# Sending the 63-row group of a top-2 gating kernel ahead of the 65-row group

## The chip, the core and the metric

The kernel runs on one core of a Trainium2 chip. The metric is the device time of one execution in microseconds (us). Before the change the median of three runs is 240.05 us (240.04, 240.05 and 240.24).

## What is computed

For each of 16 x 1024 = 16,384 tokens there are 8 router logits and a row of 512 floats. The two largest logits give two weights, and the row is written out twice, once times each weight, the smaller weight first.

```python
def reference(x, router_logits, k):            # x 16x1024x512, logits 16x1024x8, k = 2
    probs = np.exp(router_logits - logits_max)
    probs = probs / np.sum(probs, axis=-1, keepdims=True)
    topk_indices = np.argsort(probs, axis=-1)[..., -k:]
    topk_probs = np.take_along_axis(probs, topk_indices, axis=-1)
    topk_probs = topk_probs / np.sum(topk_probs, axis=-1, keepdims=True)
    x_expanded = x[:, :, np.newaxis, :].repeat(k, axis=2)
    return (x_expanded * topk_probs[..., np.newaxis]).astype(np.float32)
```

So 33.55 MB of rows and 0.52 MB of logits are read, and 67.11 MB are written. Normalising two of the eight probabilities leaves a sigmoid of the difference of the two largest logits, which is how the kernel has it.

## The kernel before

The 16,384 tokens lie on 128 partitions, 128 tokens ("rows" from here on, 2 KB each) to a partition. They are taken in two groups, the first of 65 rows per partition, the second of 63 (`GROUPS`, L49). A group is a contiguous stretch of the tensors, so a partition's rows of one group are contiguous in HBM. There is one input buffer `xs` of 65 rows per partition, which serves both groups, and one output buffer `osp` of 16 rows (each twice, for the two weights).

**Loads.** `LOADS` (L51) cuts each group's load into pieces, issued on the SyncE (SP) queue by L112: 2, 4, 2, 8, 17 and 32 rows for the first group, 16, 16 and 31 for the second. After the first 6 rows the logits of both groups are loaded by two transfers (L116, L117), and the weights `WA` of all 128 rows are worked out at once by `top2_weights` (VectorE, then two sigmoids on ScalarE).

**Products.** For each step of a plan VectorE multiplies n rows by their two weights (L128) and the result is stored by one transfer (L136), again on SP; only the first step of 2 rows is stored from ScalarE's queue. The steps of a group, as (first row, rows, target), are:

- rows 0 to 15 into `osp` (in the first group as 2 and 14 rows, in the second as 16);
- rows 16 to 31, written over `xs` rows 0 to 31, which are spent by then;
- rows 32 to 39 into the lower half of `osp`, rows 40 to 47 into its upper half;
- the rest, from row 48 on, written over the last part of `xs`, by the helper `over`, whose first target row is a = 2r - G for a group of G rows: the doubled rows end at row G.

`LAST` (L54) cuts that rest. With G = 65 it is 9 rows at 48 (target rows 31 to 48) and 8 rows at 57 (target rows 49 to 64): the first of these touches row 31, which the store of rows 0 to 31 still reads, so it waits for that store. With G = 63 it is one step of 15 rows at 48, whose target is rows 33 to 62 and touches nothing that is being stored.

**Order.** VectorE runs its steps in the order of the plan. SP issues in the order of the program and a transfer that waits holds up all behind it: the loads of the first group, its stores, the loads of the second group, its stores. A load of the second group waits until the stores have read what it overwrites: the first for the store of `xs` rows 0 to 31, the second in addition for the 9-row store (row 31), the third for the last store.

Of the kernel before, what the change touches and what calls it, by code (L numbers as in the profile page):

```python
# [1 line left out]

# [4 lines left out]

F32 = mybir.dt.float32
ALU = mybir.AluOpType
ACTF = mybir.ActivationFunctionType  # L10
P = 128


def top2_weights(nc, pool, logits, M, E, tag=""):

    hi, lo, n = None, None, E  # L20
    while n > 1:
        n //= 2
        if hi is None:
            a, b = logits[:, :, 0:n], logits[:, :, n : 2 * n]
            nhi = pool.tile([P, M, n], F32, tag=f"hi{n}{tag}")
            nlo = b
            nc.vector.tensor_tensor(nhi, a, b, op=ALU.max)  # L27
            nc.vector.tensor_tensor(nlo, a, b, op=ALU.min)  # L28
        else:
            a, b = hi[:, :, 0:n], hi[:, :, n : 2 * n]  # L30
            nhi = pool.tile([P, M, n], F32, tag=f"hi{n}{tag}")
            nlo = pool.tile([P, M, n], F32, tag=f"lo{n}{tag}")
            tmp = pool.tile([P, M, n], F32, tag=f"tmp{n}{tag}")
            nc.vector.tensor_tensor(tmp, lo[:, :, 0:n], lo[:, :, n : 2 * n], op=ALU.max)  # L34
            nc.vector.tensor_tensor(nlo, a, b, op=ALU.min)  # L35
            nc.vector.tensor_tensor(nlo, nlo, tmp, op=ALU.max)  # L36
            nc.vector.tensor_tensor(nhi, a, b, op=ALU.max)  # L37
        hi, lo = nhi, nlo
    dlt = pool.tile([P, M], F32, tag=f"dlt{tag}")
    nc.vector.tensor_tensor(dlt, hi[:, :, 0], lo[:, :, 0], op=ALU.subtract)  # L40
    WA = pool.tile([P, M, 2], F32, tag=f"WA{tag}")
    nc.scalar.activation(WA[:, :, 0], dlt, ACTF.Sigmoid, scale=-1.0)  # L42
    nc.scalar.activation(WA[:, :, 1], dlt, ACTF.Sigmoid, scale=1.0)  # L43
    return WA

GROUPS = [65, 63]  # L49

LOADS = [[2, 4, 2, 8, 17, 32], [16, 16, 31]]  # L51


LAST = [[(48, 9), (57, 8)], [(48, 15)]]  # L54


@with_exitstack
def kernel(
    ctx: ExitStack,
    tc: tile.TileContext,  # L60
    x: bass.AP,
    router_logits: bass.AP,
    k: bass.AP,
    out: bass.AP,
):
    nc = tc.nc
    B, S, D = x.shape
    E = router_logits.shape[-1]
    N = B * S
    assert int(k) == 2 and E == 8 and N == P * sum(GROUPS)  # L70
    M = N // P

    L = 16
    x_v, o_v, rl_v = [], [], []
    t0 = 0
    for n in GROUPS:
        t1 = t0 + P * n
        x_v.append(
            x.rearrange("b s d -> (b s) d")[t0:t1].rearrange("(p m) d -> p m d", p=P)
        )  # L80
        o_v.append(
            out.rearrange("b s k d -> (b s) k d")[t0:t1].rearrange(
                "(p m) k d -> p m k d", p=P
            )
        )
        rl_v.append(
            router_logits.rearrange("b s e -> (b s) e")[t0:t1].rearrange(
                "(p m) e -> p m e", p=P
            )
        )  # L90
        t0 = t1

    wpool = ctx.enter_context(tc.tile_pool(name="wpool", bufs=1))
    logits = wpool.tile([P, M, E], F32)
    xs = wpool.tile([P, max(GROUPS), D], F32)
    osp = wpool.tile([P, L, 2, D], F32)

    def over(r, n, G):

        a = 2 * r - G
        return xs[:, a : a + 2 * n, :].rearrange("p (r k) d -> p r k d", k=2)

    h = L // 2
    e = 2
    m0 = 0
    for g, G in enumerate(GROUPS):
        r = 0  # L110
        for n in LOADS[g]:
            nc.sync.dma_start(xs[:, r : r + n, :], x_v[g][:, r : r + n, :])  # L112
            r += n
            if g == 0 and r == 6:

                nc.sync.dma_start(logits[:, :G], rl_v[0])  # L116
                nc.sync.dma_start(logits[:, G:], rl_v[1])  # L117
                WA = top2_weights(nc, wpool, logits, M, E)
        assert r == G
        begin = [(0, e, osp[:, :e]), (e, L - e, osp[:, e:])] if g == 0 else [(0, L, osp)]  # L120
        plan = begin + [
            (L, L, over(L, L, 2 * L)),
            (2 * L, h, osp[:, :h]),
            (2 * L + h, h, osp[:, h:]),
        ]
        plan += [(r, n, over(r, n, G)) for r, n in LAST[g]]
        for r, n, og in plan:
            nc.vector.tensor_tensor(  # L128
                og,
                xs[:, r : r + n, :].unsqueeze(2).to_broadcast([P, n, 2, D]),  # L130
                WA[:, m0 + r : m0 + r + n, :].unsqueeze(3).to_broadcast([P, n, 2, D]),
                op=ALU.mult,
            )

            queue = nc.scalar if n == e else nc.sync
            queue.dma_start(o_v[g][:, r : r + n], og)  # L136
        m0 += G


# [1 line left out]
_INS = ['x', 'router_logits', 'k']  # L141
_OUTS = [((16, 1024, 2, 512), 'float32')]

_NUMBERS = {'k': 2}


# [26 lines left out]
```

## Time and profile before

| quantity | value |
|---|---|
| median of three runs | 240.05 us |
| span of the profiled execution | 238.5 us |
| VectorE busy | 142.0 us, 60% of the span |
| share of the SP queue's transfers in the time of 16 DMA engines | 97.8% |
| share of ScalarE's queue in it | 1.0% |
| moved | 101.19 MB |
| multiply of 8 / 9 / 15 / 16 rows (L128) | 8.69 / 9.76 / 16.16 / 17.23 us |

The span is measured from the first to the last event that the profiler ascribes to the program; the time of a run includes some 1.5 us around it. A transfer's "us to landing" runs from its issue by the queue to the moment at which its semaphore is complete. In the timeline a line merges instructions of one kind: start, length, engine and line, what is written and read, and in brackets how long the engine had been idle and who ended that. "SPq" is the issuing sequencer of SyncE, "DVE" VectorE, "ACT" ScalarE.

### The profile page before, as it was taken

How to read it: one execution, taken by the hardware profiler on the slowest of the kernel's cores; microseconds unless marked ns; L12 is line 12 of the kernel's file. 1: busy time of each engine (PE TensorE's matmuls, PEld its weight loads, DVE VectorE, ACT ScalarE, POOL GpSimd, SP SyncE). 2: the span in 40 equal slices, each digit the busy share in tenths (PEclk: the TensorE clock that was granted, in tenths of full speed). 3: DMA queues.
4: the chain of work that ended last, by engine and by line, in shares of the span. 5: the costliest groups of instructions: out<-in, count | busy, mean ns of one | idle time of the engine just before them, and what ended most of it. 6: DMA issues, size and time to landing. Idle time of an engine off the chain costs nothing.

```text
span 238.5 us, 116 instructions
## 1 busy us (share of the span) xinstructions
DVE 142.0 (60%) x23; ACT 1.8 (1%) x3; POOL 0.2 (0%) x4
## 2 busy tenths in 40 slices
DVE  0599999900299699900000699999006999990000
ACT  2000000000000000000000000000000000000000
POOL 0000000000000000000000000000000000000000
DMA  7999989899898999999999999998999989999994
GB/s 261 434 470 411 459 383 528 330 462 462 352 506 352 440 440 440 440 414 465 440 429 434 412 478 458 394 495 374 462 418 429 451 363 429 440 440 429 495 453 206
DMA packets 3312, 101.19 MB, mean 424 GB/s; under 512 B 368, under 2 KB 496, under 8 KB 880
## 3 DMA queue, kind: packets, MB, share of 16 engines
q1 hardware_dynamic: 3168, 100.14, 97.8%
q10 hardware_dynamic: 144, 1.05, 1.0%
HBM read 34.08 MB, written 67.11 MB: 424 GB/s over the span
## 4 chain that ended last, share of the span: by engine, by line
DMA 43%; DVE 41%; issue 4%; SPq 1%; ACT 0%; DVEq 0%
DVE xs L128 22%; DVE osp L128 18%; DMA out_dram<-xs 15%; DMA xs<-in_x_dram 13%; DMA out_dram<-osp 13%; DMA logits<-in_router_logits_dram 3%; SPq L112 0%; DVE nhi L27 0%; DVE logits L28 0%; DVE nlo L36 0%; DVE nhi L37 0%; DVE tmp L34 0%; DVE nlo L35 0%; SPq L116 0%; SPq L136 0%
## 5 line engine op out<-in xcount | busy, mean ns | idle before, releaser
L128 DVE TENSOR_TENSOR osp<-xs,WA 128x8192 f32<-128x8192 f32 (+3 forms) x7 | 69.1, 9908 | 61.9 <-DMA xs<-in_x_dram 31.2
L128 DVE TENSOR_TENSOR xs<-xs,WA 128x16384 f32<-128x16384 f32 (+3 forms) x5 | 69.1, 13812 | 2.2 <-DMA out_dram<-xs 2.0
L27 DVE TENSOR_TENSOR nhi<-logits 128x512 f32<-128x512 f32 x1 | 0.7, 691 | 8.3 <-DMA logits<-in_router_logits_dram 8.3
L42 ACT ACT_TABLE_LOAD x1 | 1.3, 1283 | 0.7 <-PEq L154 0.7
L28 DVE TENSOR_TENSOR logits<-logits 128x512 f32<-128x512 f32 x1 | 0.7, 692 | 0.0
L37 DVE TENSOR_TENSOR nhi<-nhi 128x256 f32<-128x256 f32 (+1 forms) x2 | 0.7, 351 | 0.0
L35 DVE TENSOR_TENSOR nlo<-nhi 128x256 f32<-128x256 f32 (+1 forms) x2 | 0.7, 350 | 0.0
L36 DVE TENSOR_TENSOR nlo<-nlo,tmp 128x256 f32<-128x256 f32 (+1 forms) x2 | 0.7, 350 | 0.0
L34 DVE TENSOR_TENSOR tmp<-logits 128x256 f32<-128x256 f32 x1 | 0.4, 418 | 0.0
L42 ACT ACTIVATE WA<-dlt 128x128 f32<-128x128 f32 x1 | 0.3, 315 | 10.2 <-DVE dlt L40 10.2
L40 DVE TENSOR_TENSOR dlt<-nhi,nlo 128x128 f32<-128x128 f32 x1 | 0.3, 291 | 0.0
L43 ACT ACTIVATE WA<-dlt 128x128 f32<-128x128 f32 x1 | 0.3, 297 | 0.0
L34 DVE TENSOR_TENSOR tmp<-nlo 128x128 f32<-128x128 f32 x1 | 0.3, 283 | 0.0
L154 POOL MEMSET const-bfloat16-1.0<- 128x1 bf16 x1 | 0.1, 101 | 0.0
L154 POOL MEMSET const-uint8-127<- 128x1 uint8 x1 | 0.1, 101 | 0.0
L154 POOL MEMSET const-float32-0.0<- 128x1 f32 x1 | 0.1, 98 | 0.2 <-issue 0.2
L154 POOL MEMSET const-float32-1.0<- 128x1 f32 x1 | 0.1, 98 | 0.0
## 6 DMA issues: line engine op xcount, KB each, us to landing
out_dram<-osp SPq DMA_DIRECT2D x4, 4096.0 KB, 20.7
xs<-in_x_dram SPq DMA_DIRECT2D x2, 4096.0 KB, 29.9
xs<-in_x_dram SPq DMA_DIRECT2D x1, 7936.0 KB, 38.0
out_dram<-xs SPq DMA_DIRECT2D x1, 7680.0 KB, 23.2
out_dram<-osp SPq DMA_DIRECT2D x1, 7168.0 KB, 33.9
out_dram<-xs SPq DMA_DIRECT2D x1, 4608.0 KB, 20.4
xs<-in_x_dram SPq DMA_DIRECT2D x1, 4352.0 KB, 22.4
out_dram<-xs SPq DMA_DIRECT2D x1, 4096.0 KB, 21.5
```

Of the source, the lines that this page charges most:

```text
L27: nc.vector.tensor_tensor(nhi, a, b, op=ALU.max)
L28: nc.vector.tensor_tensor(nlo, a, b, op=ALU.min)
L34: nc.vector.tensor_tensor(tmp, lo[:, :, 0:n], lo[:, :, n : 2 * n], op=ALU.max)
L35: nc.vector.tensor_tensor(nlo, a, b, op=ALU.min)
L36: nc.vector.tensor_tensor(nlo, nlo, tmp, op=ALU.max)
L37: nc.vector.tensor_tensor(nhi, a, b, op=ALU.max)
L40: nc.vector.tensor_tensor(dlt, hi[:, :, 0], lo[:, :, 0], op=ALU.subtract)
L42: nc.scalar.activation(WA[:, :, 0], dlt, ACTF.Sigmoid, scale=-1.0)
L43: nc.scalar.activation(WA[:, :, 1], dlt, ACTF.Sigmoid, scale=1.0)
L128: nc.vector.tensor_tensor(og, xs[:, r : r + n, :].unsqueeze(2).to_broadcast([P, n, 2, D]), WA[:, m0 + r : m0 + r + n, :].unsqueeze(3).to_b ...
L154: nc = _bacc.Bacc("TRN2", target_bir_lowering=False, num_devices=1)
```

## The change

The two groups change places: 63 rows come first and 65 second. The lists that belong to a group go with it: `LAST` is swapped as it stands, so the 15-row step now ends the first group and the 9- and 8-row steps end the second. The loads of the first group are 2, 4, 2, 8, 16 and 31 rows, those of the second 16, 17 and 32. The number of transfers, the bytes and the number of VectorE instructions stay as they were.

```diff
-GROUPS = [65, 63]
+GROUPS = [63, 65]
 
-LOADS = [[2, 4, 2, 8, 17, 32], [16, 16, 31]]
+LOADS = [[2, 4, 2, 8, 16, 31], [16, 17, 32]]
 
 
-LAST = [[(48, 9), (57, 8)], [(48, 15)]]
+LAST = [[(48, 15)], [(48, 9), (57, 8)]]
```

## The prediction

> **What bounds the kernel now.** I read the page's head first, then windows of the span, then the timeline and the landings of the transfers, and the chain of waits last.
>
> ```profile
> span 238.5 us, 116 instructions
> DVE 142.0 (60%) x23; ACT 1.8 (1%) x3; POOL 0.2 (0%) x4
> ...
> q1 hardware_dynamic: 3168, 100.14, 97.8%
> q10 hardware_dynamic: 144, 1.05, 1.0%
> ...
> DMA 43%; DVE 41%; issue 4%; SPq 1%; ACT 0%; DVEq 0%
> ```
>
> VectorE has 40% of the span free; the two DMA queues together fill 98.8% of the time of 16 DMA engines. The windows (length, engines, granted clock, DMA share, GB/s) say where the rest is:
>
> ```profile
> 0.00:1.70 1.70, 0.00 (x0) 0.97 (x1) 0.20 (x4) 1.00 0.00 0
> 47.00:142.60 95.60, 45.62 (x6) 0.00 (x0) 0.00 (x0) 1.00 1.00 434
> 43.00:47.00 4.00, 4.00 (x1) 0.00 (x0) 0.00 (x0) 1.00 1.30 492
> 158.00:162.00 4.00, 4.00 (x1) 0.00 (x0) 0.00 (x0) 1.00 1.21 516
> 236.50:238.50 2.00, 0.00 (x0) 0.00 (x0) 0.00 (x0) 1.00 0.00 0
> ```
>
> Nothing moves in the first 1.7 us, then the engines are full to the end. Packets are booked where they start, so in a short window the figures run above 1.00; what tells is share per GB/s. In the long window it is 1.00 for 434. In 43 to 47, where the first group's loads give way to its stores, 492 GB/s should take 1.13 and take 1.30: (1.30 - 1.13) x 4.0 = 0.66 us of all engines lost. At the second such turn, 158 to 162, 516 should take 1.19 and take 1.21: 0.08 us.
>
> ```profile
> 64.02 17.29 DVE L128 TENSOR_TENSOR osp<-xs,WA 128x8192 f32<-128x8192 f32 x2 [16.71 <-DMA out_dram<-osp]
> 72.74 8.93 SPq L136 DMA_DIRECT2D out_dram<-osp  x2
> 83.36 18.48 DVE L128 TENSOR_TENSOR xs<-xs,WA 128x9216 f32<-128x9216 f32 x2 [2.05 <-DMA out_dram<-xs]
> ...
> 180.91 17.29 DVE L128 TENSOR_TENSOR osp<-xs,WA 128x8192 f32<-128x8192 f32 x2 [13.39 <-DMA out_dram<-osp]
> 189.63 8.93 SPq L136 DMA_DIRECT2D out_dram<-osp  x2
> 198.24 16.16 DVE L128 TENSOR_TENSOR xs<-xs,WA 128x15360 f32<-128x15360 f32 x1
> 214.42 0.33 SPq L136 DMA_DIRECT2D out_dram<-xs  x1
> ```
>
> Issue plus time to landing gives each transfer's landing:
>
> ```profile
> out_dram<-xs SPq DMA_DIRECT2D x1, 7680.0 KB, 23.2
> out_dram<-osp SPq DMA_DIRECT2D x1, 7168.0 KB, 33.9
> xs<-in_x_dram SPq DMA_DIRECT2D x1, 7936.0 KB, 38.0
> xs<-in_x_dram SPq DMA_DIRECT2D x1, 42.6
> ```
>
> The 32-row load lands at 4.4 + 42.6 = 47.0, the 14-row store at 30.07 + 33.9 = 63.9, and so on in the order of issue: 83.2, 92.9, 102.6, 113.5 (9 rows), 123.4, 132.9 (load of 16), 142.6, 161.4 (load of 31), 180.8, 200.2, 209.8, 219.5, and the last 15-row store at 214.4 + 23.2 = 237.6. From 47.0 to 237.6, 126 rows per partition are stored and 63 loaded, 82.6 MB in 190.6 us: 433 GB/s, the rate of the full window. So one row costs 0.605 us to load and 1.210 us to store, and no transfer there waits for its issue. The kernel is bound by bytes. The chain of waits books 41% on VectorE only because each store was released by VectorE; the engines were still on earlier bytes then.
>
> **What the change removes, adds and moves.** Bytes, the 23 transfers of SP and ScalarE, and the multiplies are the same before and after, so the stream costs what it cost, unless it runs dry. That has to be looked at transfer by transfer, from the row prices above and the multiplies of the profile.
>
> First group. The two logits transfers swap their sizes (260 and 252 KB); VectorE's first instruction waits for both, so nothing moves there. The loads end 2 rows earlier, 47.0 - 1.2 = 45.8. The 14-row store, ready at 30.1, lands at 62.7 (+16.9), the 16-row store (ready at 47.3) at 82.1 (+19.4). The landing at 62.7 frees `osp`; with the 0.08 us seen between landing (63.94) and start (64.02) VectorE does the two 8-row steps from 62.8 to 80.1 (17.29 as one group). Their stores are issued at 71.5 and 80.1, are reached at 82.1 and 91.7, and land at 91.7 and 101.4. Next comes the moved step of 15 rows. The 2.05 us wait that stood here belonged to the 9-row step, whose target includes `xs` row 31; rows 33 to 62 are in no transfer. So it starts at 80.13, ends 16.16 us later, and its store is issued at 96.3. The stream gets there at 101.4: a margin of 5.1 us, the thinnest of the new order.
>
> Does 5.1 suffice? The old kernel has the same place with the same margin: its 15-row store is issued at 214.4 while the store before it lands at 198.2 + 21.3 = 219.5, and it lands 18.1 us after that, exactly 15 x 1.210. No gap. The time from an issue to moving bytes is not shown under load; bounds are 1.0 us (first issue at 0.73, DMA share zero until 1.70) and 2.4 us (the first 512 KB load lands 3.6 us after its issue, of which 1.2 are its bytes). I take 1.0, with the engines running; with 2.4 the margin is still 2.7.
>
> The Trainium skill ("DMA: Bandwidth & Descriptors", section "Anatomy of one DMA — SWDGE (gpsimd) path") would speak against longer transfers that others wait for: it gives every DMA a fixed part of about 2.0 us on that path, mostly the receipt of the last write. Twelve stores would then pay 24 us if nothing hid it; here their landings follow each other at the price of their bytes alone, so it is hidden, and at 2.0 us the 15-row store would keep 3.1 us.
>
> The second group's loads. On SP they stand behind the 15-row store. The first (16 rows) waits for the 16-row store of `xs`, landed at 82.1, so it goes at once after 96.3 (before: 102.3, behind the 8-row store). The second (17 rows) overwrites rows 16 to 32, and row 32 was read by the 8-row step that ended by 71.5: no wait left, where before it stood until 113.5 for the 9-row store. The third (32 rows, 33 to 64) waits for the 15-row store: 101.4 + 18.1 = 119.6. Behind it on SP stand only stores that are not ready before 146. At 119.6 the queue holds 33 rows of loads, 20.0 us (before: 19.1 us, 142.6 - 123.5). Landings: 129.2, 139.5, 158.9.
>
> Second group. VectorE starts 0.12 us after the 129.2 landing (as 132.91 to 133.03) and needs 17.23 twice: stores issued at 146.6 and 163.8, reached at 158.9 and 178.3, landing at 178.3 and 197.6. The 8-row steps run from 178.4 to 195.7; their stores are reached at 197.6 and 207.3, 10.5 and 11.6 us after their issue, and land at 207.3 and 217.0. Now the 9-row step waits for row 31, until 197.6: from 195.7 that is 2.0 us, so the old wait is not removed but moved here. It ends at 207.5; the stream wants it at 217.0, 9.5 us later. The 8-row step is issued at 216.2, wanted at 227.9. Last landing: 217.0 + 10.9 + 9.7 = 237.6, as before.
>
> So of the moved parts, the 2.0 us wait, the earlier loads and the shorter last store (8 rows, 9.7 us, instead of 18.1) each come out at zero, covered by margins of 5.1 to 20 us of bytes already queued. Without that cover the dearest, the 15-row multiply, would show its whole 16.2 us. The sum is 237.6 for the last landing and the same 0.9 us behind it: span 238.5, and with the 1.55 us between span and median, 240.05.
>
> What is left is the ramp. From 1.75 to 47.0 pass 45.25 us for 65 rows loaded, 2 stored and 0.52 MB of logits, 18.6 MB or 43.0 us: 2.3 us are lost there, 0.66 of them at the turn. The change cuts these loads by one row in two places; I take this loss as it is, and price its part at the turn below.
>
> **Rivals.** First, faster: the chain of waits is right, and VectorE's path sets the end; then the 2.05 us ahead of 83.36 are gained, 238.0. For it speaks only the 41% of the chain; against it the landings spaced by bytes alone, and that the wait returns at 195.7.
>
> Second, faster: the turn from loads to stores in the first group loses 0.08 instead of 0.66, because its last load is now the 31-row one that turned cheaply at 158 to 162. 240.05 - 0.58 = 239.5. Against it: the turn at 158 was the second store stream on this queue, and being first may be the cause, which the change leaves.
>
> Third, slower: the reverse. The 32-row load, after which 0.66 us were lost, now stands ahead of the second group's stores at 158.9, and if that turn loses 0.66 in place of 0.08 while the first keeps its loss, 240.05 + 0.58 = 240.6. It decides as soon as more than 0.48 us is lost there beyond today's 0.08.
>
> Fourth, slower: the stream runs dry at 101.4. It begins to cost once the 15-row store is issued later than about 100.4 (101.4 less 1.0 us). If its multiply were held until the 8-row store ahead lands, at 91.7, it would be issued at 108.0 and cost 7.6 us: 247.6. Nothing in the targets makes it wait so.
>
> **How the numbers follow.** A difference of 0.2%, 0.48 us, is what a measurement can tell from none. No change, bound by bytes: 0.76, at 240.05, with a range of its own of 239.8 to 240.3. Second rival 0.08, first 0.03, third 0.09, fourth 0.04. The range reaches from 239.6 to 240.6, half into the second and third; beyond lies about 0.15. Faster 0.11, same 0.76, slower 0.13.
>
> **What would show it.** Right: DMA share still 1.00 at 434 GB/s from 47 to 236; the 15-row step without a wait ahead of it; 2.0 us of idle time on `xs` late in the second group, at about 196; the last landing at 237.6. Wrong: stores that land later than their bytes allow after the one before, above all the 15-row one (119.6) and the first after the 32-row load (178.3), or a share per GB/s above 1.00 for 434 at the second turn.

## The result and the profile after

The changed kernel takes 240.63 us (median of 22 runs, 240.13 to 242.12); the kernel before, measured beside it 22 times, 240.26 us (240.04 to 241.18). The ratio is 1.0021, 95% interval 1.0011 to 1.0031: slower by 0.2%, half a microsecond at the mean. The medians hide its shape. Of the changed kernel's runs 9 of 22 lie above 240.7 us, of the old one's 2 of 22, and the fastest runs are equal to 0.1 us. The change makes a slower outcome more frequent; it does not add the same amount to every run.

The page of one execution of the changed kernel, which took 241.0 us:

```profile
span 239.2 us, 114 instructions
...
DVE 142.0 (59%) x23; ACT 1.8 (1%) x3; POOL 0.2 (0%) x4
...
q1 hardware_dynamic: 3168, 100.14, 97.6%
q10 hardware_dynamic: 144, 1.05, 1.0%
```

Busy time, packets and bytes are those of before; the span is 0.7 us longer. The timeline around the two places that the prediction followed:

```profile
63.13 17.29 DVE L128 TENSOR_TENSOR osp<-xs,WA 128x8192 f32<-128x8192 f32 x2 [15.54 <-DMA out_dram<-osp]
71.85 8.94 SPq L136 DMA_DIRECT2D out_dram<-osp  x2
80.46 16.16 DVE L128 TENSOR_TENSOR xs<-xs,WA 128x15360 f32<-128x15360 f32 x1
96.64 0.33 SPq L136 DMA_DIRECT2D out_dram<-xs  x1
97.03 23.34 SPq L112 DMA_DIRECT2D xs<-in_x_dram  x3
...
198.49 18.48 DVE L128 TENSOR_TENSOR xs<-xs,WA 128x9216 f32<-128x9216 f32 x2 [2.03 <-issue]
208.27 9.06 SPq L136 DMA_DIRECT2D out_dram<-xs  x2
```

The 15-row step follows the 8-row steps without a wait, and the 2.0 us wait has moved to 198.49. Landings, from issue and time to landing (the 31-row load issued at 4.63; the 15-row store at 96.64; the loads of 16, 17 and 32 rows at 97.03, 98.05 and 120.04; the last store at 217.00):

```profile
xs<-in_x_dram SPq DMA_DIRECT2D x1, 7936.0 KB, 41.5
out_dram<-xs SPq DMA_DIRECT2D x1, 7680.0 KB, 23.4
xs<-in_x_dram SPq DMA_DIRECT2D x1, 4096.0 KB, 32.7
xs<-in_x_dram SPq DMA_DIRECT2D x1, 4352.0 KB, 42.0
xs<-in_x_dram SPq DMA_DIRECT2D x1, 39.7
out_dram<-xs SPq DMA_DIRECT2D x1, 4096.0 KB, 21.3
```

Against the forecast they are 46.1 (45.8), 120.0 (119.6), 129.7 (129.2) and 140.0 us (139.5); the 32-row load lands at 159.7 (158.9), the last store at 238.3 (237.6). So 0.3 us are lost by the end of the first loads, a little at 120, and 0.3 more between 140 and 159.7. From there on the 0.7 to 0.8 us stand unchanged for 78 us of stores.

Windows of the changed kernel (length, engines, granted clock, DMA share, GB/s), first three long enough to weigh share against rate, then some so short that each counts packets, booked where they start:

```profile
42.00:46.00 4.00, 4.00 (x1) 0.00 (x0) 0.00 (x0) 1.00 1.24 483
46.10:139.60 93.50, 44.69 (x5) 0.00 (x0) 0.00 (x0) 1.00 1.01 436
155.50:159.50 4.00, 4.00 (x1) 0.00 (x0) 0.00 (x0) 1.00 1.29 524
44.95:45.45 0.50, 0.50 (x1) 0.00 (x0) 0.00 (x0) 1.00 3.98 1720
45.70:45.80 0.10, 0.10 (x1) 0.00 (x0) 0.00 (x0) 1.00 1.33 573
158.25:158.90 0.65, 0.65 (x1) 0.00 (x0) 0.00 (x0) 1.00 3.50 1512
159.35:159.45 0.10, 0.10 (x1) 0.00 (x0) 0.00 (x0) 1.00 1.52 655
235.60:236.25 0.65, 0.00 (x0) 0.00 (x0) 0.00 (x0) 1.00 1.75 756
236.70:236.80 0.10, 0.00 (x0) 0.00 (x0) 0.00 (x0) 1.00 0.76 328
```

The same of before, where the first stores and the last store's last packets start:

```profile
46.15:46.66 0.51, 0.51 (x1) 0.00 (x0) 0.00 (x0) 1.00 4.17 1799
234.25:234.85 0.60, 0.00 (x0) 0.00 (x0) 0.00 (x0) 1.00 3.54 1536
234.85:235.05 0.20, 0.00 (x0) 0.00 (x0) 0.00 (x0) 1.00 0.71 307
```

The first turn loses (1.24 - 483/434) x 4.0 = 0.5 us of all engines (before 0.66), the second (1.29 - 524/434) x 4.0 = 0.3 (before 0.08). The short windows say who pays. The first store has packets of 57,344 bytes: 1720 GB/s x 0.50 us are 15 of them, and 573 x 0.10 one. Fifteen engines begin their stores by 45.45 us and one only at 45.7. At the second turn 15 begin by 158.90 and one after 159.35; at the last store (32,768 bytes) 15 begin their last packet by 236.25, and one after 236.70. One engine is behind, falls back further in the second group's loads, and carries the gap unchanged through all stores. (The packet records carry no engine number; that it is the same engine each time is inferred.) Before, all 16 begin the first store within 0.51 us, and at the end 15 begin their last packet in one window of 0.60 us and the last one in the 0.20 us after it.

### The profile page after: what moved, and what is told of

Read it like the earlier page. It is cut to its first block, busy times and chain, and to the rows that moved or that the text cites. A ratio compares the mean times of both kernels' runs of the same rounds, so it can differ in the third digit from the quotient of the medians.

```text
span 239.2 us, 114 instructions
## 1 busy us (share of the span) xinstructions
DVE 142.0 (59%) x23; ACT 1.8 (1%) x3; POOL 0.2 (0%) x4
## 4 chain that ended last, share of the span: by engine, by line
DVE 45%; DMA 43%; issue 1%; SPq 1%; ACT 0%; DVEq 0%
DVE xs L128 22%; DVE osp L128 21%; DMA xs<-in_x_dram 14%; DMA out_dram<-osp 14%; DMA out_dram<-xs 13%; DMA logits<-in_router_logits_dram 3%; SPq L112 0%; DVE nhi L27 0%; DVE logits L28 0%; DVE nlo L36 0%; DVE nhi L37 0%; DVE tmp L34 0%; DVE nlo L35 0%; SPq L116 0%; SPq L136 0%
```

## The experiments

"Spread" below is the time from the first to the last of the 16 engines, taken from the packet records of one execution at the start of the first stores and at the end of the last; "its time" is that execution's own. A ratio is to the kernel before, with its 95% interval. Before has spreads of 0.45 and 0.70 us, after 0.79 and 1.12.

### Is it the size of the last load, or the place in HBM?

e1: the order of before with the change's last load; e2: the changed order with the last load of before.

```diff
 e1  GROUPS = [65, 63]
-LOADS = [[2, 4, 2, 8, 17, 32], [16, 16, 31]]
+LOADS = [[2, 4, 2, 8, 17, 32], [16, 15, 32]]
 e2  GROUPS = [63, 65]
-LOADS = [[2, 4, 2, 8, 16, 31], [16, 17, 32]]
+LOADS = [[2, 4, 2, 8, 16, 31], [16, 18, 31]]
```

> The order of before (65 rows first), but the second group loads 16, 15 and 32 rows instead of 16, 16 and 31, so that its last load has the size that the change put there. Theory 'size' (the loss at the second turn from loads to stores grows with the last load's packets, 64 KB instead of 62 KB): the turn near 158 us loses about 0.3 us instead of 0.08, ratio to before 1.001 to 1.002. Theory 'place' (it comes from where the 65-row group lies in HBM): turn as in before, ratio 1.000. Theory 'chance' (the loss at a turn differs from run to run whatever the order): ratio 1.000 within its interval, the turn anywhere from 0.05 to 0.7.

Measured: 1.0002 (0.9992 to 1.0012), 240.39 us; the second turn lost 0.14 us, spread 0.52 at the end.

> The changed order (63 rows first), but the second group loads 16, 18 and 31 rows instead of 16, 17 and 32. Theory 'size': the turn near 158 us loses under 0.1 us as in before, ratio to before 1.000 to 1.001. Theory 'place': the turn keeps a loss of about 0.3 us, ratio 1.002. The second load now waits for the 15-row store (about 120 us) with 16 rows of loads, 9.7 us, still queued behind it, so the stream should not run dry; if it does, the second load lands later than 11 us after the first.

Measured: 1.0014 (1.0003 to 1.0026), 240.61 us. The second load landed 10.9 us after the first, the price of its 18 rows, so the stream did not run dry. Together the two speak against 'size': the large last load costs nothing that can be told in the old order, and the small one leaves the changed order slower. In the single profiles the second turn does look as 'size' would have it (0.14 and 0.07 us), but e2's profiled run was its fastest (240.32).

e4: the last load of the changed kernel cut in two.

```diff
-LOADS = [[2, 4, 2, 8, 16, 31], [16, 17, 32]]
+LOADS = [[2, 4, 2, 8, 16, 31], [16, 17, 16, 16]]
```

> The changed order, with the last load of the second group cut into 16 and 16 rows (32 KB packets, one transfer more). Theory 'size': the stretched last packets are half as long, the second turn loses half or less (0.15 us), ratio 1.000 to 1.001. Theory 'place' or a price per turn that does not depend on the packet: still 0.3 us, ratio 1.002. An extra transfer by itself should cost nothing while the queue is full.

Measured: 1.0004 (0.9992 to 1.0016), 240.43 us, 4 of 12 runs above 240.7. The profiled run (240.75) lost 0.11 us at the turn, yet had one engine behind (spread 0.85, then 1.15). Not conclusive.

e3: the changed order, but the 63-row group lies behind the 65-row group in the tensors.

```diff
-    t0 = 0
-    for n in GROUPS:
+    for g, n in enumerate(GROUPS):
+        t0 = P * GROUPS[1] if g == 0 else 0
         t1 = t0 + P * n
...
-        t0 = t1
```

> The changed order, loads and steps, but each group keeps the place in HBM that a group of its size had in before: the 65-row group lies in the first part of the tensors and is done second. Theory 'place': as before, ratio 1.000, the second turn under 0.1 us. Theory 'size': as after, ratio 1.002, second turn about 0.3 us. If the loss follows the addresses of the first group instead, the first turn changes from 0.5 us.

Measured: 1.0024 (1.0011 to 1.0036), 241.05 us, 8 of 12 runs above 240.7. So the loss does not come from the addresses at which the groups begin. What e3 keeps of the change, besides its schedule, is the step from one partition's rows to the next: 63 rows (129,024 bytes) in the group loaded first, 65 (133,120) in the second.

### Schedule or layout?

The two were then taken apart: p1 has the changed schedule over the old layout, p2 the old schedule over the changed layout. `PLACE` cuts the tensors, `pieces` finds a step's rows in them; a step that crosses the cut becomes two transfers.

```diff
+PLACE = [65, 63]                                             # p2: [63, 65]
+SEGS = [[(0, 63, 0, 0)], [(0, 2, 0, 63), (2, 63, 1, 0)]]     # p2: [[(0, 63, 0, 0), (63, 2, 1, 0)], [(0, 63, 1, 2)]]
+    def pieces(g, r, n):
+        for s, m, part, at in SEGS[g]:
+            lo, hi = max(r, s), min(r + n, s + m)
+            if lo < hi:
+                yield lo, hi, part, at + lo - s
...
-            nc.sync.dma_start(xs[:, r : r + n, :], x_v[g][:, r : r + n, :])
+            for lo, hi, part, at in pieces(g, r, n):
+                nc.sync.dma_start(xs[:, lo:hi, :], x_v[part][:, at : at + hi - lo, :])
```

> The schedule of the change (63 rows first, its steps and loads), but every row lies in HBM as in before: a partition's rows in the first part are 65 rows apart-to-apart (133,120 bytes), and the two rows of each that the first group leaves out are loaded and stored with the second group, by one more load and one more store of 2 rows. Theory 'layout' (the first group's loads run unevenly over the 16 engines because of the 129,024-byte step between partitions): as before, ratio 1.000, spread of the engines at the last store 0.5 to 0.7 us. Theory 'schedule' (sizes and order of the loads make it): as after, ratio 1.002, spread above 1 us. Theory 'chance': ratio 1.000 to 1.002 with single times on both sides of 240.7 in either kernel.

Measured: 1.0002 (0.9992 to 1.0012), 240.28 us, none of 12 runs above 240.7, spread 0.55 and 0.50.

> The reverse: the schedule of before (65 rows first), but every row lies in HBM as in after (129,024 bytes from partition to partition in the first part, the 252 KB of logits first); the first group's last two rows come from the second part by one more load and one more store. Theory 'layout': ratio 1.002, single times above 240.7 in 4 of 10 runs, loads of the first group uneven, spread at the last store above 1 us. Theory 'schedule': ratio 1.000, few runs above 240.7, spread 0.5 to 0.7 us.

Measured: 1.0019 (1.0005 to 1.0033), 240.69 us, 6 of 12 runs above 240.7. Its profiled run (240.22) was its fastest, and has a spread of only 0.60 at the end; so this profile does not show what its later runs lost. By the times, the schedule is cleared and the layout carries the loss. Each of the two has one load and one store more than the kernel before, so that an extra transfer does not explain why they differ; timed side by side, their means are 0.44 us apart.

f64: two groups of 64 rows.

```diff
-GROUPS = [63, 65]
+GROUPS = [64, 64]
-LOADS = [[2, 4, 2, 8, 16, 31], [16, 17, 32]]
+LOADS = [[2, 4, 2, 8, 16, 32], [16, 16, 32]]
-LAST = [[(48, 15)], [(48, 9), (57, 8)]]
+LAST = [[(48, 16)], [(48, 16)]]
```

> Two groups of 64 rows: no wait of the last step on the 16-row store in either group, and 131,072 bytes from partition to partition in both parts. Same bytes, one store less than before. Theory 'layout': the step between partitions matters, so this one differs from both, 1.003 or more if an even power of two is worse. Theory 'schedule' (last load of 32 rows ahead of the turn): about 1.001 to 1.002 as after.

Measured: 1.0036 (1.0020 to 1.0052), 241.06 us, all 12 runs above 240.7. Its page and its last store, with the same reading as above (65,536-byte packets):

```profile
span 239.3 us, 112 instructions
...
q1 hardware_dynamic: 3024, 100.14, 97.7%
q10 hardware_dynamic: 144, 1.05, 1.0%
...
234.55:235.25 0.70, 0.00 (x0) 0.00 (x0) 0.00 (x0) 1.00 3.24 1404
235.55:235.65 0.10, 0.00 (x0) 0.00 (x0) 0.00 (x0) 1.00 1.51 655
```

Again 15 engines by 235.25 and one 0.3 us behind. But that is the smaller part: the packets took 98.7% of 239.3 = 236.2 us per engine, against 98.8% of 238.5 = 235.6 before, so some 0.5 us fell on the average of all 16. With a step of 128 KB exactly, every run is above 240.7.

g1: the changed kernel with the logits first.

```diff
-            nc.sync.dma_start(xs[:, r : r + n, :], x_v[g][:, r : r + n, :])
-            r += n
-            if g == 0 and r == 6:
+            if g == 0 and r == 0:
                 nc.sync.dma_start(logits[:, :G], rl_v[0])
...
+            nc.sync.dma_start(xs[:, r : r + n, :], x_v[g][:, r : r + n, :])
+            r += n
```

> The changed kernel with the two logits transfers issued ahead of the first load of x instead of after 6 rows. If the loss begins in the very first transfers (the first load landed at 4.61 us in after and 4.38 in before, and every later landing is later by as much), a different first transfer takes it away or moves it: ratio 1.000, first logits at about 3.5 us. If it comes from the larger loads alone: ratio 1.002 and the spread grows as in after. VectorE starts earlier, by some 3 us, which should be worth nothing.

Measured: 1.0057 (1.0034 to 1.0079), 241.83 us over 6 runs: worse, against both expectations. The first logits landed at 3.7 us and VectorE began at 4.5 instead of 8.6, which was worth nothing. The lag was there by the first stores: the spread is 1.8 us at them and 2.0 at the end. The window of its first stores has 14 engines by 46.50 and the last one after 46.90:

```profile
span 240.2 us, 115 instructions
...
q1 hardware_dynamic: 3168, 100.14, 97.2%
q10 hardware_dynamic: 144, 1.05, 1.0%
...
45.10:46.50 1.40, 1.40 (x1) 0.00 (x0) 0.00 (x0) 1.00 1.33 573
46.90:47.00 0.10, 0.10 (x1) 0.00 (x0) 0.00 (x0) 1.00 1.33 573
```

The packets' own time is 235.9 us per engine in g1 (98.2% of 240.2) and in after (98.6% of 239.2) alike, yet g1's last engine ends 1.0 us later. This is the plainest showing that the end is the slowest engine's, and that a lag made at the start lasts.

### Which transfers?

q1 swaps the two logits transfers of the changed kernel; q2 stores as before, q3 loads x as before, each with all else as changed (`PLACE` for x, output and logits apart); q4 has the schedule of before on tensors cut at 72 and 56 rows.

```diff
 q1
-                nc.sync.dma_start(logits[:, :G], rl_v[0])
                 nc.sync.dma_start(logits[:, G:], rl_v[1])
+                nc.sync.dma_start(logits[:, :G], rl_v[0])
 q2
+PLACE_X, PLACE_O, PLACE_L = [63, 65], [65, 63], [63, 65]
...
 q3
+PLACE_X, PLACE_O, PLACE_L = [65, 63], [63, 65], [63, 65]
...
 q4
+PLACE_X, PLACE_O, PLACE_L = [72, 56], [72, 56], [72, 56]
...
```

> The changed kernel with its two logits transfers issued in the other order, 260 KB first and then 252 KB, as in before. Theory 'step of x' (the 129,024 bytes between the partitions' rows in the first group's loads): nothing changes, ratio 1.002. Theory 'logits' (the size of the first logits transfer, the other part of the layout): ratio 1.000.

> The changed kernel, its loads of x and logits as they are, but the stores laid out as in before (133,120 x 2 bytes from partition to partition for the group done first, and the split store of 2 and 14 rows for the second). So the rows go to other tokens' places in the output. Theory 'loads' (the step of the first group's loads): ratio 1.002. Theory 'stores' (the step of its stores): ratio 1.000.

> The reverse: x loaded as in before (133,120 bytes from partition to partition for the group done first, the second group's first load split in 2 and 14 rows), logits and stores as in the changed kernel. So some rows get other tokens' weights and places. Theory 'loads': ratio 1.000, the best case of the three. Theories 'stores' and 'logits': ratio 1.002.

> The schedule of before, but the tensors are cut into 72 and 56 rows per partition: the first group takes 65 of the 72 (147,456 bytes from partition to partition), the other 7 come with the second group by one more load and one more store. Theory 'near 128 KB' (a step close to 131,072 bytes makes the first loads uneven, 64 rows worst): as good as before or better, ratio 0.999 to 1.000. Theory 'only 65 is good': above 1.001. If the spread of the engines at the last store falls to 0.4 us, 0.2 us are to be gained.

Measured: q1 1.0011 (1.0000 to 1.0023), q2 1.0010 (0.9995 to 1.0024), q3 0.9993 (0.9984 to 1.0003), q4 0.9993 (0.9983 to 1.0004); runs above 240.7: 5 of 12, 3 of 12, 0 of 11, 0 of 11. With the loads of x as before the loss is gone, with stores and logits as before (p1) or as changed (q3); with the loads as changed, logits or stores laid out as before do not clearly take it away. q1 and q2 by themselves are too close to their intervals to exclude a share of either. In q4 all 16 engines begin their last packet (61,440 bytes) within half a microsecond:

```profile
234.35:234.85 0.50, 0.00 (x0) 0.00 (x0) 0.00 (x0) 1.00 4.53 1966
```

Neither q4 nor q3 is shown to beat the kernel before: both intervals reach past 1.

### The first group's loads alone

Four kernels keep the logits, the weights, six loads of the same 63 rows and the first product and store; only the step differs, 63, 64, 65 or 72 rows (`GROUPS = [63, 65]` to `[72, 56]`).

> The first group's loads alone: logits, weights, the same 63 rows per partition as six loads, and the first product and store of 2 rows; all other products, loads and stores are left out. Step between partitions 63 rows. Bytes 17.1 + 0.5 + 1.0 MB, some 18.1 MB, 41.8 us at 433 GB/s and about 5 us around it. Theory 'loads alone': 0.2 to 0.4 us slower than s65 and s72 at the median, single times spread over 1 us. Theory 'needs the turns': as s65 within 0.1 us.

> As s63, step of 64 rows. Theory 'loads alone': the slowest of the four, 0.3 us or more behind s65. Theory 'needs the turns': all four within 0.1 us.

> As s63, step of 65 rows (133,120 bytes). Theory 'loads alone': with s72 the fastest, little spread. Theory 'needs the turns': all four within 0.1 us.

> As s63, step of 72 rows (147,456 bytes). Theory 'loads alone': as s65 or faster by 0.1 us. Theory 'needs the turns': all four within 0.1 us.

Measured: 47.83, 47.92, 47.83 and 48.02 us (4 or 5 runs each, within 47.67 to 48.16). No slower 63, and 72 is last. 'Loads alone' falls: the step makes no difference that follows the full kernels when nothing stands behind the loads. 'Needs the turns' did not come true to the letter either, as the four lie 0.19 us apart and not within 0.1. (63 rows per partition are 16.5 MB, which is what the expected 18.1 MB are added up from.)

### The first group or the second?

A first group at 63 had so far come with a second at 65. v1 loads both at a step of 65, v2 both at 63; all else is the changed kernel, but for one load more in v2.

```diff
 v1
+    x_v[0] = x_f[: P * 65].rearrange("(p m) d -> p m d", p=P)
 v2
+    x_v[1] = x_f[P * 65 :].rearrange("(p m) d -> p m d", p=P)
...
+                    nc.sync.dma_start(xs[:, 0:2, :], x_v[0][:, 0:2, :])
```

> The changed kernel, its second group as it is (rows 65 apart from partition to partition), but the first group's 63 rows are loaded at a step of 65 as well, so that some of them are other tokens' rows; no transfer more or less. Theory 'first group' (the loss comes with the step of its loads): ratio 1.000, spread of the engines at the first stores 0.45 to 0.55 us. Theory 'second group' (a step of 65 in the loads ahead of the second turn): ratio 1.002, spread grows by 0.2 to 0.4 us at that turn.

> The changed kernel, its first group as it is (63), but the second group's rows are loaded at a step of 63 (2 of them from the first part by one more load), so that they are other tokens' rows. Theory 'first group': ratio 1.002. Theory 'second group': ratio 1.000, the spread does not grow at the second turn. If both kernels lie at 1.001, each group has a share.

Measured: v1 1.0006 (0.9995 to 1.0018), v2 1.0007 (0.9996 to 1.0018), 3 and 2 of 12 runs above 240.7. Both lie between the two kernels, as a share of each group would have it, but both intervals also hold 1.000 and nearly 1.002, so this is not settled. Nor do the spreads decide: from the first to the last stores v1's grows from 0.40 to 0.53 us and v2's from 0.54 to 0.74, while 'second group' had 0.2 to 0.4 more in v1 and no growth in v2.

## Why the prediction was wrong

**The forecast** was no change at 240.05, range 239.6 to 240.6, with 0.13 for slower. Measured were 240.63 and a change beyond its interval. Some 0.2 us of the miss are in the base: the three runs at hand had a median of 240.05, and 22 runs give 240.26. The term "the 1.55 us between span and median" was mis-sized by as much, as are the 1.5 us given for it ahead of the prediction: it sets the span of one execution against the time of another. In every later execution the time is 1.7 to 1.8 us above its own span (after: 241.0 and 239.2), so the profile of 238.5 us belongs to the run of 240.24, and the same sum with 1.8 us gives 240.3.

**What held.** The schedule came out as worked out. The 15-row store was issued at 96.6 (forecast 96.3), the store ahead of it landed at 101.7, so the margin was 5.1 as forecast, and it landed 18.3 us later (18.1). The wait on row 31 moved to the second group with 2.0 us and cost nothing. The loads' waits that went away and the shorter last store gave nothing. From 46 to 139.6 us the engines ran at 436 GB/s with share 1.01. The fourth rival did not happen, and p1 shows by its time that the new schedule is free within its interval: 1.0002 (0.9992 to 1.0012). The first rival (VectorE's path sets the end) fell: VectorE began the second group at 129.9 instead of 133.0 us, and the run was no shorter for it.

**The step that failed** is the sentence "The kernel is bound by bytes", carried on to "the stream costs what it cost, unless it runs dry", and with it "I take this loss as it is" of the ramp: the sum has no term for where the rows lie in HBM. The same bytes did not cost the same. By the queue shares of the two pages the packets took 98.8% of 238.5 = 235.6 us per engine before and 98.6% of 239.2 = 235.9 after, some 0.3 us more on the average of the 16, and the last engine ended 1.12 us behind the first instead of 0.70; together these make the 0.7 us of the span (of two single executions, of 241.0 and 240.24 us). The packet records show it in the loads. From 50 to 96 us and after 165, where only stores run, all packets of one size took the same time in both kernels (32,768 bytes 1.213 us, 65,536 bytes 2.418 us), and the lag neither grew nor shrank there. Packets of the loads were stretched instead: at the first turn up to 3.20 us where others of their size took 2.42 before, and up to 3.04 (2.34) after; at the second up to 2.66 (2.34) before and 3.03 (2.42) after. The schedule was examined for a dry stream, while the change also altered where every row of the first and second group lies: 63 instead of 65 rows from one partition to the next. That it did was in the code before (`rearrange("(p m) d -> p m d", p=P)` over P x n rows), and the forecast priced only the lengths of the loads. The times place the loss in that layout of the loads: 1.0019 with the new layout under the old schedule (p2), 1.0002 and 0.9993 with the loads laid out as before under the new one (p1, q3).

**The third rival** named the place and nearly the price: the second turn lost 0.3 instead of 0.08 us in the profiled run, and its 240.6 is the measured median, in part by luck, since 0.2 us of that are the base. And its mechanism, the 32-row load, did not stand: e1 has that load and is at 1.0002, e2 does without it and is at 1.0014. And only half of what after's profiled run lost lies there; 0.3 us were gone by 46 us, 0.2 of them at the landing of the very first load (4.6 us instead of 4.4).

How the end follows the spread, over the profiled runs:

| kernel | steps of the loads, first / second group | ratio | runs above 240.7 | spread at first / last stores, us | its time, us |
|---|---|---|---|---|---|
| q4 | 72 / 56 | 0.9993 | 0 of 11 | 0.43 / 0.43 | 240.09 |
| p1 | 65 / 63 | 1.0002 | 0 of 12 | 0.55 / 0.50 | 240.06 |
| e1 | 65 / 63 | 1.0002 | 2 of 12 | 0.44 / 0.52 | 240.45 |
| q3 | 65 / 63 | 0.9993 | 0 of 11 | 0.76 / 0.83 | 240.35 |
| p2 | 63 / 65 | 1.0019 | 6 of 12 | 0.47 / 0.60 | 240.22 |
| e2 | 63 / 65 | 1.0014 | 5 of 12 | 0.58 / 0.72 | 240.32 |
| after | 63 / 65 | 1.0021 | 9 of 22 | 0.79 / 1.12 | 241.00 |
| e3 | 63 / 65 | 1.0024 | 8 of 12 | 0.76 / 1.21 | 240.96 |
| e4 | 63 / 65 | 1.0004 | 4 of 12 | 0.85 / 1.15 | 240.75 |
| q1 | 63 / 65 | 1.0011 | 5 of 12 | 0.53 / 0.76 | 240.42 |
| q2 | 63 / 65 | 1.0010 | 3 of 12 | 0.53 / 0.68 | 240.17 |
| v1 | 65 / 65 | 1.0006 | 3 of 12 | 0.40 / 0.53 | 240.19 |
| v2 | 63 / 63 | 1.0007 | 2 of 12 | 0.54 / 0.74 | 240.26 |
| f64 | 64 / 64 | 1.0036 | 12 of 12 | 0.71 / 0.99 | 241.08 |
| g1 | 63 / 65 | 1.0057 | 6 of 6 | 1.82 / 2.05 | 241.96 |

Profiled runs with a spread under 0.9 at the last stores took at most 240.45, those of 0.99 or more 240.75 (e4) to 241.96. Over the seven kernels with loads at 63 and then 65 and the logits after 6 rows, 40 of 94 runs lie above 240.7; over e1, p1 and q3, 2 of 35. The kernel before is not free of such runs: over all the rounds it has 21 of 153, and 4 of 9 (up to 242.30) in the round of the loads alone.

**What stays open.** That the layout of the loads carries the loss rests on the times of many runs; the profiles show how it is paid, in load packets that take longer, on the average of the engines and most on one. The changed kernel itself was timed in one round only and the rounds ran on several chips, so kernels of different rounds are compared through the kernel before. q3 and q4 have a load more than after, as p1 and p2 have; in v1, which loads the first group at 65 without one, the loss is not clearly gone. Why loads at 63 and then 65 rows, or at 64, bring slow runs more often is not shown: the loads alone do not do it, which engine it is the records do not tell, and first and second group were not separated beyond their intervals.

The Trainium skill ("DMA: Bandwidth & Descriptors", section "Latency and other measured facts") reports for copies between HBM tensors 207 GB/s at a step of 512 KiB between partitions, 164 at 2 MiB and 103 at 4 MiB, and 214 when the 4 MiB step is padded by 4 KiB; it calls the cause, partitions in lockstep on one HBM channel, an inference. No run here has so large a step. The step of exactly 128 KiB has the highest ratio of those tried with the logits after 6 rows, but by 0.36%, and loads at 63 rows and then 65 (2 KiB short of it, then 2 KiB beyond) are slower than at 65 and then 63. The section "The descriptor swizzle" of that page gives each engine a fixed set of 8 partitions in a 128-partition transfer, on trn2 for transfers issued from SP too. No run here shows which engine serves which partitions; with such a fixed share, an engine that lags could not be relieved by the others, as the unchanged gap from 159 to 237 us has it.

## What to carry to other kernels

In these runs the end of a full transfer stream was that of its slowest engine, so look at the spread of the 16 engines and at the time their packets took, not only at bytes and gaps: count the packets that start in windows of a few tenths of a microsecond at the first and the last store. A change of tiling that looks like an exchange of sizes also moves the rows in memory; price the step between partitions as a part of the change, and test it by laying the old addresses under the new schedule. Where single runs spread over 2 us, three runs of before fix the base no better than the effect sought here; and a span goes with the time of its own execution, not with a median.

## What was not expected of the hardware

A lag of one engine, made in the loads, was kept to a hundredth of a microsecond through 78 us of stores in both before and after (spread 0.70 and 1.12 us at the second turn and at the end); only in e1 did it shrink clearly, from 0.77 to 0.52. The first turn from loads to stores costs all engines 0.4 to 0.7 us in the full kernels (nothing in g1, whose engines were already 1.8 us apart), the second 0.0 to 0.3. Putting 0.5 MB of logits ahead of the first rows, which let VectorE begin 4 us earlier, set the engines 1.8 us apart and cost 0.57%.
